# Two layers of a diffusion backbone on one core: adaLN sums on three elementwise engines instead of fp32 strip matmuls

## Chip, cores and metric

The kernel runs on one core of one Trainium2 chip. The metric is the device time of one execution in microseconds; given are the median and the range of three runs. A profile is one execution recorded by the hardware profiler. PE is TensorE (its matmuls) and PEld its weight loads, DVE is VectorE, ACT is ScalarE, POOL is GpSimd, SP is SyncE, which issues most DMAs.

## What is computed

512 latent tokens and 256 context tokens, 1024 wide, go through two layers in fp32. Each layer forms shift, scale and gate from a conditioning vector (adaLN), normalises its input, projects it, mixes tokens by attention, gates with SiLU, projects out and adds the result to the stream.

```python
def adaln(cvec, w, b):
    m = jax.nn.silu(cvec) @ w + b
    return jnp.split(m, 3, axis=-1)

for i in range(DEPTH):                      # DEPTH = 2
    shift, scale, gate = adaln(c, ada_w[i], ada_b[i])
    cshift, cscale, cgate = adaln(c_ctx, ada_w[i], ada_b[i])
    h = rms_norm(x, pre_g[i]) * (1.0 + scale) + shift
    hc = rms_norm(xc, pre_g[i]) * (1.0 + cscale) + cshift
    # i = 0: differential attention, 8 heads; i = 1: grouped-query attention, 8 heads, 2 kv heads
    x = x + gate * rms_norm(y, post_g[i])
    # layer 0 only: xc = xc + cgate * rms_norm(yc, post_g[i])
```

The part that the change touches is the product of the two vectors silu(c) and silu(c_ctx) with `ada_w`: 1024 rows in, 3072 columns out, for each layer. The columns are taken in sections of 512: 0 and 1 are shift, 2 and 3 scale, 4 and 5 gate. The projections and attention products are written as three products of a high and a low part (hi*hi, hi*lo, lo*hi), in a rounded fp32 form that TensorE takes in one pass.

## The kernel before

Layer 0's shift and scale are made first, since the first projections need them; this part stays as it is. While layer 0's heads run, the kernel makes six more sections in the order of the tuple `SECS`: layer 0's gate (0,4) and (0,5), then layer 1's shift and scale (1,0), (1,2), (1,1), (1,3). Layer 1's gate is made later, in layer 1's heads, by running sums on DVE (`gate1_part`, L1598: acc = row tile times a scalar per partition, plus acc) and a column sum on PE (`colsum`, L406 and L407).

Each of the six sections was made in two groups. `grp_load` (L826) fetches four k tiles of 128 x 512, 1 MB in one DMA on SP's queue, into one buffer `araw`. `grp_mm` (L836) multiplies each of the four by a 128 x 32 block `s32`, whose first two columns are the two vectors, so that the four results lie in four strips of 32 partitions of one PSUM bank. These are true fp32 matmuls, two passes each. The first group of a section is copied to `arow` by ACT (L839), the second added by DVE (L842). Then `gate0_finish` (gate) splits the row in a high and a low part (L1128, L1129) and multiplies by a selector `selb` that picks one vector's row out of each strip, adds them and spreads them over all partitions (L1132, L1134); `ada1_finish` (shift, scale) transposes four 128 x 128 blocks on PE (`row_cols`, L532), adds the strips on DVE (L536) and writes `mods`.

The order of the work comes from a planner. `flow` holds streams of steps with due times: scores and softmax (`S_`), transposes of p (`T_`), p times v (`M_`), sub-layer norms (`X_`), and the adaLN steps (`A_`). It runs what is due on a clock of estimated costs, and fills up with pieces of the projections from `fillq`. `ACCN` says how many adaLN steps belong to each head. The constants at the head of the file (lags, priorities, orders of projections, choice of engine) feed it, and a scheduler then places every instruction in its engine's queue, which runs in order.

For one tile of 128 queries in layer 0, per head: PE writes scores to PSUM (L995), DVE takes the maximum (L1000), ACT the exponential p (L1003), DVE the reciprocal of the sum (L1006), GpSimd scales the first map's p (L233), DVE adds the second map's with its factor (L1011), PE transposes p (L1060), ACT and DVE split it into ah and al (L1063, L1064), PE multiplies by v (L167). Weights come through `raw` buffers on SP's queue (L223), are rounded to whi by ACT (L225) and their rests wlo made by DVE (L219).

Of the kernel before, what the change touches and what calls it, by code (L numbers as in the profile page):

```python
# [61 lines left out]
EHL = ('vvvvvvvv', 'pppppppp')
EWL = ('vp', 'vp', 'pp', 'pp')
XF = (0, 0, 0)
FL = (2, 3, 2)
RB = 1
# [21 lines left out]
def tile_backbone(  # L88
# [401 lines left out]
    sel32 = cp.tile([P, 2], F32, name="sel32", bufs=1)  # L490
    nc.vector.tensor_reduce(sel32, ident.rearrange("p (j r) -> p r j", j=4)[:, 0:2, :], AX.X, ALU.add)
    selb = [cp.tile([P, P], F32R, name=f"selb{v}", bufs=1) for v in range(2)]
    for v in range(2):
        nc.vector.tensor_copy(selb[v], sel32[:, v:v + 1].to_broadcast([P, P]))
# [33 lines left out]
    def row_cols(r, n):  # L528
        o = scb[:, 0, :n * P] if seq else trp()[:, :n * P]
        for b in range(n):  # L530
            with after(seq[0] if seq else None):
                i = nc.tensor.transpose(o[:, b * P:(b + 1) * P], r[:, b * P:(b + 1) * P], ident)  # L532
# [3 lines left out]
        nc.vector.tensor_reduce(  # L536
            cols_.rearrange("p (b r) -> p b r", b=n), o.rearrange("p (b j r) -> p b r j", j=4, r=32)[:, :, 0:2, :], AX.X, ALU.add)
        return cols_
# [277 lines left out]

    with tc.tile_pool(name="t0", bufs=1) as t0:
        SECS = ((0, 4), (0, 5), (1, 0), (1, 2), (1, 1), (1, 3))
        groups = [(layer, sec, g) for layer, sec in SECS for g in range(2)]
        loaded, rows = {}, {}  # L820

        def grp_load(i):
            if i < len(groups):
                layer, sec, g = groups[i]
                t = loaded[i] = t0.tile([P, 4, 512], F32, tag="araw", name=nm("araw"), bufs=1)
                nc.sync.dma_start(  # L826
                    t, ada_w[layer, g * 512:(g + 1) * 512, sec * 512:(sec + 1) * 512].rearrange("(k p) n -> p k n", p=P))

        def grp_mm(i):
            layer, sec, g = groups[i]  # L830
            t = loaded.pop(i)
            o = trp()
            prev = None
            for j in range(4):
                with onward(prev):
                    prev = nc.tensor.matmul(o[32 * j:32 * j + 32, :], s32[:, 4 * g + j, :], t[:, j, :], start=True, stop=True)  # L836
            if g == 0:
                r = rows[layer, sec] = t0.tile([P, 512], F32, tag="arow", name=nm("arow"), bufs=1)
                nc.scalar.copy(r, o)  # L839
            else:  # L840
                r = rows[layer, sec]
                nc.vector.tensor_tensor(r, o, r, ALU.add)  # L842
            grp_load(i + 1)

        def ada1_finish(layer, sec):
            r = rows.pop((layer, sec))
            ov_ = row_cols(r, 4).rearrange("p (k v) -> p v k", v=2)
            mod_cols(layer, sec % 2, sec // 2, lambda v: ov_[:, v, :])
# [271 lines left out]
        gate0 = [hp.tile([P, D], F32, name=f"gate0_{v}", bufs=1) for v in range(2)]  # L1120

        def gate0_finish(half):
            r = rows.pop((0, 4 + half))
# [3 lines left out]
            rh, rl = (t0.tile([P, 512], F32R, tag="tmp", name=nm("rg"), bufs=3) for _ in range(2))  # L1127
            nc.scalar.copy(rh, r)  # L1128
            nc.vector.tensor_tensor(rl, r, f32(rh), ALU.subtract)  # L1129
            for v in range(2):  # L1130
                o = trp()
                nc.tensor.matmul(o, selb[v], rh, start=True, stop=False)  # L1132
                with tc.high_priority(offset=3000):
                    nc.tensor.matmul(o, selb[v], rl, start=False, stop=True)  # L1134
# [31 lines left out]
            add({"qk": qk_proj, "v": v_proj, "z": z_proj}[kind](i))  # L1166
        def acc_steps():
            res = []
            grp_load(0)
            for i, (layer, sec, g) in enumerate(groups):  # L1170
                res.append(Step(lambda i=i: grp_mm(i), 1.5, hot=False))
                if g:
                    f = (lambda sec=sec: gate0_finish(sec - 4)) if layer == 0 else (lambda layer=layer, sec=sec: ada1_finish(layer, sec))
                    res.append(Step(f, 2.0 if layer == 0 else 1.0, [(res[-1], ACD)], hot=False))
# [637 lines left out]
```

## Time and profile before

| what | value |
|---|---|
| runs, median (range) | 787.72 us (787.7 to 788.16) |
| profiled execution, first to last instruction | 786.1 us |
| PE busy | 771.3 us |
| PEld busy | 683.3 us |
| DVE busy | 526.6 us |
| ACT busy | 452.0 us |
| POOL busy | 321.8 us |
| granted TensorE clock, mean | 0.998 |

A line of the profile names the source line, the engine, the operation, `out<-in` by the program's names, the shape, and the count; behind the bar stand the busy time in us, the mean of one instruction in ns, and the idle time of the engine just before such instructions with what ended it. In a wait, `A <- B` means that A waited for B, with the total in us, how often, and the longest. In the timeline a line is the start, the duration, and merged instructions of one kind. Layer 0's heads run from about 80 to 455 us, its output projection to about 515, layer 1 from there to the end.

### The profile page before, as it was taken

To read this page: it belongs to the slowest core of one execution; us is meant where nothing else is said; L and a number is where in the kernel's file an instruction comes from. 1 tells how busy PE (TensorE), PEld (TensorE's weight loads), DVE (VectorE), ACT (ScalarE), POOL (GpSimd) and SP (SyncE) were. 2 spreads that over 40 slices of the span, in tenths; PEclk is the share of its full clock that TensorE was granted. 3 is DMA by queue.
4 is the path that set the end of the run, shared out by engine and by line. 5 is a ranking of instruction groups with operands and counts; after the bars stand their busy time and mean duration, and the time that the engine had idled before them with its cause. 6 is when DMAs were issued, how large, how long until landed. Compare 5 with 4: busy or idle time off the path is not lost.

```text
span 786.1 us, 13615 instructions
## 1 busy us (share of the span) xinstructions
PE 771.3 (98%) x5158; PEld 683.3 (87%) x5158; DVE 526.6 (67%) x934; ACT 452.0 (58%) x982; POOL 321.8 (41%) x428
## 2 busy tenths in 40 slices
PE   8999999999999999999999999999999999999996
PEld 6689888989888998988979888887999999989986
DVE  4666676886879747867578735667568987665634
ACT  5546546674576644774468724654466676666632
POOL 1121364663346542453425402574545555234102
PEclk9999999999999999999999999999999999999999
DMA  9925211230142421312520133031423512100102
GB/s 339 387 80 202 74 55 42 68 134 28 48 151 84 148 82 68 90 71 95 173 96 29 53 148 121 1 113 59 157 81 103 157 39 80 51 31 28 54 28 107
DMA packets 34065, 77.72 MB, mean 99 GB/s; under 512 B 3408, under 2 KB 8016, under 8 KB 34000
## 3 DMA queue, kind: packets, MB, share of 16 engines
q1 hardware_dynamic: 30144, 71.05, 26.9%
q10 hardware_dynamic: 3856, 5.81, 2.1%
q8 instruction: 40, 0.66, 0.3%
q14 instruction: 25, 0.20, 0.1%
HBM read 70.56 MB, written 2.10 MB: 92 GB/s over the span
## 4 chain that ended last, share of the span: by engine, by line
PE 93%; DVE 3%; ACT 3%; DMA 1%; issue 1%; POOL 0%; SPq 0%; DVEq 0%; ACTq 0%
PE bk L155 57%; PE sc L155 11%; PE bk L167 9%; PE sc L995 5%; PE bk L1060 3%; PE bk L1552 3%; PE bk L836 1%; PE sc L1024 1%; DMA xnt<-in_xlT 1%; ACT p L1003 1%; PE bk L406 1%; PE sc L1348 1%; PE bk L407 0%; PE bk L1488 0%; DVE wlo L219 0%
## 5 line engine op out<-in xcount | busy, mean ns | idle before, releaser
L155 PE MATMUL bk<-h,whi 128*128 128x512 f32 (+2 forms) x864 | 228.3, 347 | 0.0
L155 PE MATMUL bk<-whi,h 128*128 128x256 f32 (+1 forms) x992 | 226.0, 317 | 1.4 <-DVE kl L1422 1.4
L155 PEld LDWEIGHTS bk<-whi,h 128*128 128x128 f32 x992 | 165.8, 190 | 17.4 <-issue 3.2
L155 PEld LDWEIGHTS bk<-h,whi 128*128 128x128 f32 x864 | 149.9, 189 | 17.1 <-issue 3.3
L155 PE MATMUL bk<-wlo,h 128*128 128x256 f32 (+1 forms) x496 | 155.5, 315 | 0.0
L155 PE MATMUL bk<-h,wlo 128*128 128x512 f32 (+2 forms) x432 | 148.5, 345 | 0.0
L233 POOL TENSOR_SCALAR p<-p,sm 128x768 f32<-128x768 f32 (+1 forms) x80 | 70.5, 884 | 160.1 <-DVE sm L1006 72.9
L219 DVE TENSOR_TENSOR wlo<-raw,whi 128x1024 fp32r<-128x1024 f32 (+1 forms) x66 | 81.9, 1243 | 39.9 <-ACT whi L225 38.1
L155 PEld LDWEIGHTS bk<-wlo,h 128*128 128x128 f32 x496 | 94.0, 190 | 6.1 <-issue 0.7
L225 ACT CAST whi<-raw 128x1024 fp32r<-128x1024 f32 x64 | 67.1, 1049 | 52.0 <-PE bk L155 32.4
L155 PEld LDWEIGHTS bk<-h,wlo 128*128 128x128 f32 x432 | 81.3, 189 | 7.7 <-issue 1.1
L1003 ACT ACTIVATE p<-sc,sm 128x768 f32<-128x768 f32 (+1 forms) x68 | 59.5, 878 | 38.8 <-DVE sm L1000 38.5
L1000 DVE TENSOR_REDUCE sm<-sc 128x1 f32<-128x768 f32 (+1 forms) x68 | 60.3, 917 | 18.5 <-PE sc L995 18.3
L219 POOL TENSOR_TENSOR sz<-sz,za 128x192 f32<-128x192 f32 (+1 forms) x48 | 34.8, 745 | 68.4 <-ACT za L199 68.3
L1064 DVE TENSOR_TENSOR al<-bk,ah 128x512 fp32r<-128x512 f32 x56 | 37.3, 683 | 10.5 <-ACT ah L1063 10.3
L995 PE MATMUL sc<-qk,qk 64*128 64x384 f32 (+1 forms) x396 | 43.6, 350 | 0.7 <-ACT p L1003 0.7
L1011 DVE SCALAR_TENSOR_TENSOR p<-p,sm,p 128x768 f32<-128x768 f32 (+1 forms) x34 | 39.9, 1175 | 4.0 <-POOL p L233 1.6
L1556 DVE TENSOR_TENSOR al<-bk,ah 128x512 fp32r<-128x512 f32 x48 | 32.1, 685 | 15.5 <-ACT ah L1555 15.3
L995 PEld LDWEIGHTS sc<-qk,qk 64*128 64x128 f32 x396 | 32.8, 184 | 7.9 <-issue 3.1
L1537 ACT ACTIVATE p<-sc,sm,qrs 128x768 f32<-128x768 f32 x32 | 31.9, 998 | 11.6 <-PE bk L1552 5.2
L1063 ACT CAST ah<-bk 128x512 fp32r<-128x512 f32 x56 | 31.7, 590 | 11.6 <-PE bk L1060 10.0
L1555 ACT CAST ah<-bk 128x512 fp32r<-128x512 f32 x48 | 27.1, 589 | 18.7 <-PE bk L1552 17.4
(241 smaller groups left out, 1503.5 us busy)
## 6 DMA issues: line engine op xcount, KB each, us to landing
raw<-in_a_w SPq DMA_DIRECT2D x28, 512.0 KB, 3.6
araw<-in_ada_w SPq DMA_DIRECT2D x12, 1024.0 KB, 5.1
raw<-in_b_w SPq DMA_DIRECT2D x20, 512.0 KB, 3.5
ag<-in_ada SPq DMA_DIRECT2D x16, 512.0 KB, 7.8
raw<-in_w_out SPq DMA_DIRECT2D x16, 512.0 KB, 3.5
sw<-qr ACTq DMA_DIRECT2D x32, 128.0 KB, 2.1
gw<-in_ada_w SPq DMA_DIRECT2D x8, 512.0 KB, 3.8
xnt<-in_xlT SPq DMA_DIRECT2D x4, 512.0 KB, 5.7
```

Of the source, the lines that this page charges most:

```text
L155: i = nc.tensor.matmul(o, a, b, start=start, stop=stop)
L167: nc.tensor.matmul(o, v[:, kt + e, c], a[:, e * 256:e * 256 + 256], start=first and i == 0, stop=last and i == 5)
L219: eng.tensor_tensor(dst[:, i:i + n], a[:, i:i + n], b[:, i:i + n], op)
L225: nc.scalar.copy(hi, r)
L233: (nc.vector if eng == "v" else nc.gpsimd).tensor_scalar(dst, src, s_, 1.0, ALU.mult, ALU.mult)
L995: prev = nc.tensor.matmul(sc[m][:, j if nk == T else m, :w], a[r, tok], b[r, c], start=i == 0, stop=i == 2)
L1000: nc.vector.tensor_reduce(mx, scv, AX.XY if nk == T else AX.X, ALU.max, negate=True)
L1003: nc.scalar.activation(pv_, scv, AF.Exp, bias=mx, accum_out=l[:, m:m + 1])
L1011: nc.vector.scalar_tensor_tensor(ps_[0], pt, r, ps_[0], ALU.mult, ALU.add)
L1064: nc.vector.tensor_tensor(al, tr, f32(ah), ALU.subtract)
L1537: nc.scalar.activation(pt.rearrange("p (j n) -> p j n", j=2), scv, AF.Exp, scale=sr, bias=nmx, accum_out=l)
L1556: nc.vector.tensor_tensor(al, tr, f32(ah), ALU.subtract)
```

## The change

The six sections are no longer made by matmuls. Each comes in four parts of two k tiles (512 KB, two buffers, the load two parts ahead). For either vector `v` there is an accumulator of 128 x 512, to which every k tile times its scalar per partition is added. For the first vector all eight tiles go on DVE (one scaling, seven multiply-adds). For the second, the first tile goes on DVE, and each of the other seven is scaled in place by ACT and added by GpSimd. The sum over the 128 partitions is left to the finish. `gate0_finish` does it with `colsum` (all ones instead of the selector); the low part is now made by GpSimd. `sec_finish` transposes 32 x 32 blocks of the accumulator on DVE and reduces them, which leaves 16 numbers per partition in `rall`; when the last section is there, one fp32 matmul with `msel`, a mask and one more reduction give the columns of all four sections, and `mods` is written.

```diff
+EACC = ('dddddddd', 'daaaaaaa')
-                t = loaded[i] = t0.tile([P, 4, 512], F32, tag="araw", name=nm("araw"), bufs=1)
+                t = loaded[i] = t0.tile([P, 2, 512], F32, tag="araw", name=nm("araw"), bufs=2)
...
-            for j in range(4):
-                with onward(prev):
-                    prev = nc.tensor.matmul(o[32 * j:32 * j + 32, :], s32[:, 4 * g + j, :], t[:, j, :], start=True, stop=True)
-            if g == 0:
-                r = rows[layer, sec] = t0.tile([P, 512], F32, tag="arow", name=nm("arow"), bufs=1)
-                nc.scalar.copy(r, o)
-            else:
-                r = rows[layer, sec]
-                nc.vector.tensor_tensor(r, o, r, ALU.add)
+            for k in range(2):
+                k_ = 2 * k2 + k
+                for v in range(2):
+                    acc = sums[layer, sec][v]
+                    s_ = scol[:, v, k_:k_ + 1]
+                    e = EACC[v][k_]
+                    eng = {"d": nc.vector, "p": nc.gpsimd, "a": nc.scalar}[e]
+                    with tc.issue_after(last_of(eng)):
+                        if e == "d" and k_:
+                            eng.scalar_tensor_tensor(acc, t[:, k, :], s_, acc, ALU.mult, ALU.add)
+                            continue
+                        o = t[:, k, :] if k_ else acc
+                        if e == "a":
+                            eng.activation(o, t[:, k, :], AF.Copy, scale=s_)
+                        else:
+                            eng.tensor_scalar(o, t[:, k, :], s_, None, ALU.mult)
+                    if k_:
+                        with tc.issue_after(last_of(nc.gpsimd)):
+                            nc.gpsimd.tensor_tensor(acc, acc, o, ALU.add)
+            part_load(i + 2)
...
+        def sec_finish(layer, sec):
+            idx = 2 * SECS.index((layer, sec)) - 4
+            for v in range(2):
+                tr = t0.tile([P, 512], F32, tag="tmp", name=nm("tr"), bufs=3)
+                with tc.issue_after(last_of(nc.vector)):
+                    nc.vector.transpose(tr, sums[layer, sec][v])
+                    nc.vector.tensor_reduce(rall[:, idx + v, :], tr.rearrange("p (b i) -> p b i", i=32), AX.X, ALU.add)
+            if sec == 3:
+                o = trp()[:, :P]
+                nc.tensor.matmul(o, msel, rall.rearrange("p s b -> p (s b)"), start=True, stop=True)
...
-                nc.tensor.matmul(o, selb[v], rh, start=True, stop=False)
+                colsum(o, sums[0, 4 + half][v], [t0.tile([P, 512], F32R, tag="tmp", name=nm("rg"), bufs=3) for _ in range(2)])
```

The constants are fitted anew, some thirty-five of them. Those that move work between engines: `EG0` (gT scaled by subg, 24 instructions) from DVE to ACT, `EG1` (layer 1's copy of g, 16) from ACT to DVE, `HFD` (one more of four hf tiles on DVE), `KVE` and `EWL` (some wlo). `HF0` puts z projection 6 into the last head, `KV` reorders layer 1's k, v and transposes, `ACCN` is (1, 4, 2, 4, 6, 5, 5, 3) for 30 steps where it was (0, 0, 3, 2, 4, 1, 4, 4) for 18, `NWARM` is 11 and not 12.

PE's queue before, in head 3, around its norm's column sum (sqs); bk are PSUM banks, whi and wlo weights, h the normalised input:

```order
L155 MATMUL bk_68<-wlo_2623,h_279 128x256
L406 MATMUL bk_69<-sqs_2986,ones_r 128x384
L155 MATMUL bk_68<-whi_2622,h_280 128x256
L155 MATMUL bk_68<-whi_2622,h_327 128x256
L155 MATMUL bk_68<-wlo_2623,h_327 128x256
L836 MATMUL bk_70<-araw_2749,s_129 32x512 x4
L407 MATMUL bk_69<-sqs_2987,ones_r 128x384
```

The same column sum of head 3 on PE in the changed kernel:

```order
L156 MATMUL bk_68<-wlo_2671,h_581 128x256
L156 MATMUL bk_68<-whi_2670,h_582 128x256
L407 MATMUL bk_70<-sqs_3109,ones_r 128x384
L156 MATMUL bk_68<-whi_2670,h_591 128x256
L156 MATMUL bk_68<-wlo_2671,h_591 128x256
L156 MATMUL bk_68<-whi_2670,h_592 128x256
L156 MATMUL bk_69<-whi_2537,h_231 128x256
```

The strip group (L836) is gone; projections stand around the column sum as before, others of the same kind.

GpSimd's queue before, in head 3: p is the softmax scaling, qr the rotation of the next head's q and k, sqs the norm's low part:

```order
L233 TENSOR_SCALAR p_2832<-p_2832,sm_2817 128x768
L219 TENSOR_TENSOR qr_2629<-qr_2629,rope 128x256 x2
L219 TENSOR_TENSOR qr_2629<-qr_2629,sw_2776 128x256 x2
L233 TENSOR_SCALAR p_2941<-p_2941,sm_2926 128x768
L405 TENSOR_TENSOR sqs_2980<-sq_2772,sqs_2979 128x384
L233 TENSOR_SCALAR p_3044<-p_3044,sm_3029 128x768
L405 TENSOR_TENSOR sqs_2987<-sq_2772,sqs_2986 128x384
```

GpSimd's queue in head 3 of the changed kernel (L855 is the addition to the second vector's accumulator):

```order
L234 TENSOR_SCALAR p_2933<-p_2933,sm_2918 128x768
L406 TENSOR_TENSOR sqs_3103<-sq_2889,sqs_3102 128x384
L855 TENSOR_TENSOR acc_2829<-acc_2829,araw_2619 128x512 x2
L234 TENSOR_SCALAR p_3017<-p_3017,sm_3002 128x768
L220 TENSOR_TENSOR qr_2871<-qr_2871,rope 128x256 x2
L406 TENSOR_TENSOR sqs_3110<-sq_2889,sqs_3109 128x384
L220 TENSOR_TENSOR qr_2871<-qr_2871,sw_2984 128x256 x2
L855 TENSOR_TENSOR acc_2829<-acc_2829,araw_2835 128x512 x2
L234 TENSOR_SCALAR p_3133<-p_3133,sm_3118 128x768
L855 TENSOR_TENSOR acc_2829<-acc_2829,araw_2950 128x512 x2
L234 TENSOR_SCALAR p_3248<-p_3248,sm_3233 128x768
```

Between two scalings of p there now stands a pair of 512-wide additions, directly ahead of the next scaling.

DVE's queue in the changed kernel, head 3 (L1025 maximum, L1031 reciprocal, L1036 combination of the two maps, L220 rest of a weight tile, L846 the multiply-add to the first vector's accumulator):

```order
L1036 SCALAR_TENSOR_TENSOR p_2933<-p_2939,sm_2918,p_2933 128x768
L846 SCALAR_TENSOR_TENSOR acc_2828<-araw_2619,scol,acc_2828 128x512 x2
L1025 TENSOR_REDUCE sm_3015<-sc_72 128x1
L1025 TENSOR_REDUCE sm_3021<-sc_73 128x1
L1031 RECIPROCAL sm_3002<-sm_3002 128x1
L220 TENSOR_TENSOR wlo_3068<-raw_3065,whi_3067 128x1024
L846 SCALAR_TENSOR_TENSOR acc_2828<-araw_2835,scol,acc_2828 128x512
L1031 RECIPROCAL sm_3002<-sm_3002 128x1
L846 SCALAR_TENSOR_TENSOR acc_2828<-araw_2835,scol,acc_2828 128x512
```

The multiply-adds stand between the steps of the softmax, where before there were none of them.

More of the change, by code (lines that the diff above doesn't have):

```diff
@@ L62 @@
 EHL = ('vvvvvvvv', 'pppppppp')
[L63 to L66, printed above, removed]
+EWL = ('pv', 'vp', 'pp', 'pv')
+XF = (0, 4, 1)
+FL = (0, 1, 3)
+RB = 2
 HFB = 3
-PRI = (1359, 218, 582, 400)
+PRI = (1359, 0, 523, 648)
 GFIN = (10, 13)
-QLAG = 2.87
-QTR = 7.76
-EG0 = 'v'
+QLAG = 2.99
+QTR = 9.24
+EG0 = 'a'
 EP0 = 'p'
@@ L489, in tile_backbone @@
     nc.vector.tensor_copy(s32[:, :, 0:2], scv)
[L490 to L494, printed above, removed]
+    msel = cp.tile([P, 4, 32], F32, name="msel", bufs=1)
+    mask = cp.tile([P, 4], F32, name="mask", bufs=1)
+    nc.vector.tensor_reduce(msel[:, 0, :], ident.rearrange("p (g j) -> p j g", j=32), AX.X, ALU.add)
+    nc.vector.tensor_copy(msel[:, 1:, :], msel[:, 0:1, :].to_broadcast([P, 3, 32]))
+    nc.vector.tensor_reduce(mask, ident.rearrange("p (a r) -> p a r", r=32), AX.X, ALU.add)
+    msel = msel.rearrange("p g j -> p (g j)")
     def quad(cs, o, g):
@@ L818, in tile_backbone @@
         SECS = ((0, 4), (0, 5), (1, 0), (1, 2), (1, 1), (1, 3))
[L819 to L824, printed above, removed]
-                t = loaded[i] = t0.tile([P, 4, 512], F32, tag="araw", name=nm("araw"), bufs=1)
+        parts = [(layer, sec, k2) for layer, sec in SECS for k2 in range(4)]
+        loaded, sums = {}, {}
+        rall = con.tile([P, 8, 16], F32, name="rall")
@@ L826, in grp_load, with part_load @@
+        def part_load(i):
+            if i < len(parts):
+                layer, sec, k2 = parts[i]
+                t = loaded[i] = t0.tile([P, 2, 512], F32, tag="araw", name=nm("araw"), bufs=2)
                 nc.sync.dma_start(
-                    t, ada_w[layer, g * 512:(g + 1) * 512, sec * 512:(sec + 1) * 512].rearrange("(k p) n -> p k n", p=P))
-        def grp_mm(i):
-            layer, sec, g = groups[i]
+                    t, ada_w[layer, k2 * 256:(k2 + 1) * 256, sec * 512:(sec + 1) * 512].rearrange("(k p) n -> p k n", p=P))
@@ L843, in grp_mm @@
[L843 to L848, printed above, removed]
+            if k2 == 0:
+                sums[layer, sec] = [t0.tile([P, 512], F32, tag=f"acc{v}", name=nm("acc"), bufs=1) for v in range(2)]
+            for k in range(2):
[17 more added lines that the diff above has]
+                            nc.gpsimd.tensor_tensor(acc, acc, o, ALU.add)
@@ new lines, in part_sum_ @@
+            part_load(i + 2)
[9 more added lines that the diff above has]
+                nc.tensor.matmul(o, msel, rall.rearrange("p s b -> p (s b)"), start=True, stop=True)
+                om = con.tile([P, 32, 4], F32, name="om")
+                nc.vector.tensor_tensor(om, o.rearrange("p (s a) -> p s a", a=4), mask.unsqueeze(1).to_broadcast([P, 32, 4]), ALU.mult)
+                oc_ = con.tile([P, 4, 2, 4], F32, name="oc")
+                nc.vector.tensor_reduce(oc_.rearrange("p s v k -> p (s v k)"), om, AX.X, ALU.add)
+                for i, (l_, sc_) in enumerate(SECS[2:]):
+                    mod_cols(1, sc_ % 2, sc_ // 2, lambda v: oc_[:, i, v, :])
@@ L1168, in acc_steps @@
             res = []
[L1169 to L1174, printed above, removed]
+            part_load(0)
+            part_load(1)
+            for i, (layer, sec, k2) in enumerate(parts):
+                res.append(Step(lambda i=i: part_sum_(i), 0.0, hot=False))
+                if k2 == 3:
+                    f = (lambda sec=sec: gate0_finish(sec - 4)) if layer == 0 else (lambda layer=layer, sec=sec: sec_finish(layer, sec))
+                    res.append(Step(f, 2.0 if layer == 0 else 0.0, [(res[-1], ACD)], hot=False))
             return res
```

63 lines of the change are left out of this document (29 added, 34 removed).

## The prediction

> **What bounds the kernel now.** I read the page's head first, then the chain, then what TensorE waited for, then the stretches of the span.
>
> ```profile
> span 786.1 us, 13615 instructions
> PE 771.3 (98%) x5158; PEld 683.3 (87%) x5158; DVE 526.6 (67%) x934; ACT 452.0 (58%) x982; POOL 321.8 (41%) x428
> PE 93%; DVE 3%; ACT 3%; DMA 1%; issue 1%; POOL 0%; SPq 0%; DVEq 0%; ACTq 0%
> ```
>
> The reader is to see three things: matmuls cover 98% of the span, the chain that ended last lies on PE for 93% of it, and PE's idle time is 786.1 - 771.3 = 14.8 us in all. All eleven waits of PE for another engine stand in one answer; here are its longest, at the start of the program, and the two that lie in layer 0's heads, where the change is (us in total, times, longest):
>
> ```profile
> PE bk L155 <- DVE sqx L618: 1.8, 3, 1.2
> ...
> PE bk L167 <- DVE al L1064: 1.2, 1, 1.2
> ...
> PE bk L836 <- DVE al L1064: 0.6, 1, 0.6
> ```
>
> The stretches show where the idle time lies (columns: busy time of PE, weight loads, DVE, ACT, POOL):
>
> ```profile
> 0.00:40.00 40.00, 35.56 (x251) 26.12 (x252) 22.53 (x63) 20.83 (x42) 6.26 (x13) 1.00 0.97 358
> 120.00:440.00 320.00, 318.72 (x2296) 281.70 (x2295) 232.02 (x392) 195.71 (x417) 151.81 (x181) 1.00 0.27 88
> 400.00:440.00 40.00, 38.87 (x272) 34.69 (x273) 32.87 (x63) 29.84 (x66) 19.09 (x22) 1.00 0.16 53
> 590.00:636.00 46.00, 46.00 (x339) 44.55 (x338) 41.05 (x78) 30.55 (x67) 21.93 (x27) 1.00 0.43 125
> 760.00:786.00 26.00, 20.06 (x134) 18.41 (x132) 12.43 (x19) 7.26 (x20) 4.76 (x14) 0.94 0.26 94
> ```
>
> The first 40 us (4.4 idle) and the last 26 (5.9) hold most of it. Layer 0's heads, 120 to 440, where all strip matmuls lie, lose 1.3 us in 320. There a microsecond of PE work removed is a microsecond gained, as long as the other engines still keep up. Matmul ends are modelled, so I check with starts:
>
> ```profile
> 184.42 0.40 PE L155 MATMUL bk<-whi,h 128*128 128x256 f32 x2
> 184.66 0.28 PE L155 MATMUL bk<-wlo,h 128*128 128x256 f32 x1
> 184.78 0.28 PE L155 MATMUL bk<-whi,h 128*128 128x256 f32 x1
> ```
>
> Four 256-column matmuls start within 0.36 us, one per 0.12, with no gap: PE is really streaming. [...] The even starts speak for the full amount, which I take.
>
> **What goes from PE.** One strip group and its neighbours, and one finish of a section:
>
> ```profile
> L836 PE MATMUL bk<-araw,s 128*32 128x512 f32 x96 | 12.8, 605 | 0.6 <-DVE al L1064 0.6
> 160.12 0.40 PE L167 MATMUL bk<-al,vhi 128*128 128x256 f32 x2
> 160.45 1.07 PE L836 MATMUL bk<-araw,s 128*32 128x512 f32 x8
> 161.45 0.38 PE L155 MATMUL bk<-whi,h 128*128 128x256 f32 x1
> 161.67 0.28 PE L155 MATMUL bk<-wlo,h 128*128 128x256 f32 x1
> ...
> 302.73 0.40 PE L167 MATMUL bk<-al,vhi 128*128 128x256 f32 x2
> 302.97 0.60 PE L532 MATMUL bk<-ident,arow 128*128 128x128 f32 x4
> 303.50 1.33 PE L995 MATMUL sc<-qk,qk 64*128 64x384 f32 x12
> ```
>
> The two L167 from 160.12 would have been followed at 160.36; L155 starts at 161.45, 1.09 us later, and its successor 0.22 us after it and not 0.12. One group thus holds PE 1.19 us, and the 12 groups 14.3 us (a little over the 12.8 busy). The four transposes of a section's finish hold it from 302.97 to 303.50: 0.53, four finishes 2.1 us. What comes in is one fp32 matmul of 128 columns (two passes), for all four sections together. The nearest row is the warm-up matmul of that shape, and the two rows behind it are gate0's:
>
> ```profile
> L155 PE MATMUL sc<-ones 128*128 128x128 f32 x14 | 2.4, 297 | 0.3 <-DVE sm L536 0.3
> L1132 PE MATMUL bk<-rg,selb 128*128 128x512 f32 x4 | 1.8, 446 | 0.0
> ```
>
> 7 of them in 2.4 us are 0.34 each; I take 0.4. gate0 keeps eight matmuls of the same shape (ones for a selector), so 0. One warm-up matmul less and two fills more lie in the first 40 us, in idle time: 0, and without that cover 0.34 each. Net on PE: 14.3 + 2.1 - 0.4 = 16.0 us.
>
> **What comes to the others.** Layer 1's gate is already made by such sums on DVE; its rows and the nearest others:
>
> ```profile
> L1598 DVE SCALAR_TENSOR_TENSOR gate<-gw,scol,gate 128x512 f32<-128x512 f32 x14 | 12.3, 877 | 0.1
> L1596 DVE TENSOR_SCALAR gate<-gw,scol 128x512 f32<-128x512 f32 x2 | 1.4, 718 | 0.0
> L1030 DVE TENSOR_REDUCE sm<-sc 128x2 f32<-128x512 f32 x14 | 9.4, 683 | 2.1 <-PE sc L1024 2.1
> L233 DVE TENSOR_SCALAR gT<-bk,subg 128x256 f32<-128x256 f32 x24 | 11.5, 477 | 6.3 <-ACT sq L1081 6.3
> L842 DVE TENSOR_TENSOR arow<-bk,arow 128x512 f32<-128x512 f32 x6 | 4.1, 685 | 1.1 <-PE bk L836 0.9
> L1129 DVE TENSOR_TENSOR rg<-arow,rg 128x512 fp32r<-128x512 f32 x2 | 1.7, 840 | 0.0
> L1128 ACT CAST rg<-arow 128x512 fp32r<-128x512 f32 x2 | 1.2, 620 | 2.0 <-DVE arow L842 1.5 <-issue 0.5
> L1081 ACT ACTIVATE sq<-bk 128x256 f32<-128x256 f32 x24 | 9.3, 386 | 4.0 <-PE bk L167 3.9
> L839 ACT COPY arow<-bk 128x512 f32<-128x512 f32 x6 | 3.5, 585 | 2.2 <-PE bk L836 2.2
> L405 POOL TENSOR_TENSOR ac<-gate,ac 128x512 fp32r<-128x512 f32 x2 | 2.6, 1300 | 0.3 <-ACT ac L404 0.2
> L405 POOL TENSOR_TENSOR sqs<-sq,sqs 128x512 fp32r<-128x512 f32 x1 | 1.9, 1885 | 0.1
> ```
>
> DVE: 42 multiply-adds x 0.877 = 36.8; 12 scalings x 0.718 = 8.6; 8 block transposes, which the trace does not show, between 0.68 and 0.88 by the one-input and two-input rows of 128x512, taken at 0.72 = 5.8; 8 reductions x 0.683 = 5.5. Off it go the 24 scalings of gT that move to ACT (11.5), the L842 additions (4.1) and L1129 (1.7). Sum +39.4. ACT: 42 scalings x 0.62 = 26.0, 24 of gT x 0.386 = 9.3, two more casts 1.2, less 3.5: +33.0. GpSimd: 42 adds, between 1.3 and 1.885, taken at 1.5 = 63, and gate0's four low parts x 1.3 = 5.2: +68.
>
> Layer 0's heads then take 320 - 16 = 304 us of PE, beside DVE 232 + 39 = 271 (89%), ACT 196 + 33 = 229 (75%), GpSimd 152 + 68 = 220 (72%). The same load stands in the trace: 590 to 636, with layer 1's running sums, has DVE at 41.05 of 46 (89%) and PE without any idle time. But ACT (66%) and GpSimd (48%) were freer there. In 400 to 440, with DVE at 82% and ACT at 75%, PE lost 1.13 us of 40. So the heads' 304 us lose between 0 and 1.13 x 304/40 = 8.6 us more. I take 2.5, nearer to the first row, because the instruction is the same; this is a choice.
>
> **Waits, and what stands behind them.** On GpSimd an addition to acc now waits for ACT's scaling and for the DMA, and in the new order the softmax scaling of the next query tile stands right behind pairs of them. Who waits for that is the m=1 combination on DVE, then the transposes on PE. On SP a part's load waits until DVE and GpSimd have left its buffer, with the weight loads behind it; before, L826 waited for PE in the same way:
>
> ```profile
> SPq L826 <- PE bk L836: 59.3, 9, 11.8
> ```
>
> Yet none of PE's eleven waits is for a DMA. I cost this at 0 to 2, taken at 0. PSUM: twelve uses of a bank go, worth nothing where PE did not wait.
>
> **The rest of the refit** moves layer 1's copies of g and one more hf tile in four from ACT to DVE, reorders the k and v work, and puts one z projection a head later. From 440 on PE idles 7.8 us, of which 5.9 are the end that no order shortens much. I take 0, bounds -2 to +2.
>
> **Sum.** 786.1 - 16.0 + 2.5 = 772.6 for the span. The median of the runs, 787.72, lies 1.6 above this execution's span; so 774.2, and I forecast **774**. With the bounds: 787.72 - 16.0 - 2 = 769.7 to 787.72 - 16.0 + 8.6 + 1 = 781.3.
>
> **Rivals.**
> First, GpSimd's pairs come late for PE (chance 0.10).
>
> ```profile
> POOL p L233 <- DVE sm L1006: 72.9, 24, 8.6
> ...
> 182.78 1.01 DVE L1011 SCALAR_TENSOR_TENSOR p<-p,sm,p 128x768 f32<-128x768 f32 x1
> 185.89 0.65 PE L1060 MATMUL bk<-ident,p 128*128 128x128 f32 x4
> ```
>
> Here p was ready at 183.79 and read at 185.89: 2.1 us of cover. A pair of adds takes 2.6 at least. If each of the 24 parts reaches PE with the 0.5 left over, 12 us come back: 787.72 - 16 + 12 = 783.7. Against it: GpSimd waited 72.9 us for DVE in front of that scaling, so it has gaps to put pairs in.
>
> Second, on the other side: DVE and GpSimd hold each other up and DVE becomes the bound (0.08). Layer 1's sums show it:
>
> ```profile
> L1598 DVE SCALAR_TENSOR_TENSOR gate<-gw,scol,gate x14: 726/749/1477, 591.9 to 633.5; 128x512 f32<-128x512 f32 x14
> ```
>
> Median 0.749, longest 1.477. At 1.477 for all 42, DVE has 271 + 25 = 296 us; 89% is the highest DVE share at which the trace shows a PE without waits, and 296/0.89 = 333 us of heads instead of 320 make 787.7 + 13 = 801. It decides from 0.89 x 321.6 = 286 us of DVE work on, that is from a mean of 1.24 us. For it: GpSimd has 45% more work to collide with. Against it: 0.877 is a mean that already holds collisions. [...]
>
> Third, the freed PE time is no gain because PE's order, not its work, sets the pace (0.02): 787. The even starts speak against it. Fourth, the refit removes waits as well, below 769.5 (0.04).
>
> **How the numbers follow.** My own case has 0.76, with 769.7 to 781.3. The range, 769.5 to 783, adds about half of the first rival. Faster by over 0.2% (below 786.1; about what a measurement can tell here) gets the own case, the first and the fourth rival, less a little for a first rival that grows: 0.88. Within 0.2%: 0.04, the third rival and that remainder. Slower: 0.08.
>
> **What would show it.** In the changed profile: PE's busy time near 771.3 - 15 = 756, no strip group; the multiply-add row of acc near 0.88 us (over 1.24 the second rival); GpSimd's adds 1.3 to 1.9 us; DVE near 89% from 120 to 424 with PE's idle time there below 10 us. I am wrong if PE's waits for al, p or acc in layer 0's heads sum to over 8 us, or if layer 1 moves by more than 2.

## The result and the profile after

The changed kernel takes 806.38 us (median of four runs, 804.15 to 807.43) where the kernel before takes 787.82: a ratio of 1.0231, interval 1.0216 to 1.0247, 18.6 us slower. The forecast was 774, the far end of its range 783. One execution of one kernel below, the one with the gate's low part on DVE, took 2657 us; its median is that of the other three.

The head of its page and the chain:

```profile
span 803.7 us, 13614 instructions
PE 770.5 (96%) x5050; PEld 685.1 (85%) x5050; DVE 583.9 (73%) x991; ACT 475.6 (59%) x1022; POOL 395.6 (49%) x476
PE 26%; DVE 3%; POOL 1%; ACT 1%; DMA 1%; issue 0%; DVEq 0%; ACTq 0%; POOLq 0%
```

PE's idle time is 803.7 - 770.5 = 33.2 us where it was 14.8, and its busy time has not fallen although it holds 108 matmuls fewer (5050 for 5158). The chain's shares add up to a third of the span only, so it says little here. The stretch of layer 0's heads that the prediction argued from (columns as there; then granted clock, DMA share, GB/s):

```profile
120.00:440.00 320.00, 302.55 (x2092) 270.67 (x2089) 264.60 (x388) 212.38 (x448) 214.66 (x217) 0.98 0.27 85
```

PE lost 1.3 us there before and loses 17.4 now, at a mean clock of 0.98 instead of 1.00. DVE is at 264.60 of 320, 83%: not full. The starts of the context scores of heads 0 to 6 show how the loss gathers:

| us | 0 | 1 | 2 | 3 | 4 | 5 | 6 | last transposes of p | last matmul |
|---|---|---|---|---|---|---|---|---|---|
| before | 107 | 148 | 185 | 231 | 277 | 336 | 379 | 446 | 780 |
| after | 107 | 159 | 199 | 245 | 299 | 347 | 396 | 471 | 797 |

The distance is 0, 11, 14, 14, 22, 11 and 17 us at the heads, 25 at the last transposes of layer 0 and 17 at the end. It does not grow evenly, since projections stand between the heads in another order (a z projection is now in the last one). The 8 us that come back are not layer 1's: from the first transposes of its p to the last matmul it takes 192.9 us before and 193.8 after. They lie between the two attentions, 140.9 us before and 132.8 after. One planner constant moved by 0.1 in the kernel before (ATT, below) makes this stretch 149.1 us with the total only 1.5 us longer, so these marks do not tell how much work is done by then. What PE waited for, longest first, with one line further down:

```profile
PE sc L1020 <- ACT p L1028: 3.5, 3, 2.1
PE bk L156 <- DVE al L1089: 3.4, 3, 1.7
PE bk L408 <- POOL rg L406: 3.3, 2, 2.7
...
PE bk L1085 <- DVE al L1089: 1.2, 2, 1.0
...
PE bk L168 <- DVE al L1089: 1.0, 3, 0.6
```

No wait is large; they are many and short. The waits for al and p in the heads come to 3.5 + 3.4 + 1.2 + 1.0 = 9.1 us, over the 8 at which I said I would be wrong. The longest single one, of 2.7 us, shows how a short wait becomes a long loss. The timeline there (PE, DVE and POOL):

```profile
143.71 4.79 POOL L855 TENSOR_TENSOR acc<-acc,araw 128x512 f32<-128x512 f32 x3
145.92 1.25 DVE L1035 TENSOR_TENSOR sm<-sm,nlam 128x1 f32<-128x1 f32 x1
147.27 2.04 DVE L1036 SCALAR_TENSOR_TENSOR p<-p,sm,p 128x768 f32<-128x768 f32 x1
147.32 0.49 PE L407 MATMUL bk<-rg,ones_r 128*128 128x512 f32 x1
148.46 1.98 POOL L406 TENSOR_TENSOR rg<-acc,rg 128x512 fp32r<-128x512 f32 x1
150.49 0.50 PE L408 MATMUL bk<-rg,ones_r 128*128 128x512 f32 x1 [2.68 <-POOL rg L406]
151.75 1.01 PE L156 MATMUL bk<-h,whi 128*128 128x384 f32 x2 [0.55 <-ACT qr L892]
152.56 0.52 PE L156 MATMUL bk<-h,wlo 128*128 128x384 f32 x1
152.88 0.84 PE L156 MATMUL bk<-h,whi 128*128 128x384 f32 x2
```

Two stretches of 4 us of the same place:

```profile
148.00:152.00 4.00, 0.95 (x3) 0.52 (x4) 3.81 (x5) 1.78 (x4) 4.00 (x4) 0.86 0.41 131
152.00:156.00 4.00, 4.00 (x13) 4.00 (x14) 3.42 (x5) 1.09 (x3) 1.83 (x2) 0.50 0.40 131
```

Three additions hold GpSimd for 4.79 us. Behind them stands the low part of the gate's row (rg), 1.98 us long; PE's second column sum (L408) needs it and stands at the head of PE's queue, so nothing on PE starts for 2.68 us. Meanwhile a multiplication of 128 numbers takes DVE 1.25 us (mean before: 0.253) and the combination of p 2.04. Then the granted clock falls to 0.50: the 384-column matmuls start 0.32 us apart (152.56 to 152.88), where the commonest distance of such matmuls in this trace is 0.175. Three slices of 40 us hold such falls, where before all slices from 120 to 440 had 1.00:

```profile
120.00:160.00 40.00, 35.64 (x217) 30.54 (x215) 31.23 (x41) 22.68 (x46) 25.56 (x21) 0.91 0.19 60
...
240.00:280.00 40.00, 36.79 (x245) 31.88 (x244) 31.96 (x47) 26.31 (x58) 29.57 (x30) 0.96 0.32 103
...
360.00:400.00 40.00, 35.66 (x258) 31.67 (x258) 34.28 (x51) 25.17 (x50) 29.22 (x28) 0.96 0.38 119
```

They lose up to (0.09 + 0.04 + 0.04) x 40 = 6.8 us of full-speed time by the clock alone (up to, because PE stood idle in a little of it).

### The profile page after: what moved, and what is told of

It reads as the page before. It is cut to its first block, busy times and chain, and to the rows that moved or that the text cites. A ratio compares the mean times of both kernels' runs of the same rounds, so it can differ in the third digit from the quotient of the medians.

```text
span 803.7 us, 13614 instructions
## 1 busy us (share of the span) xinstructions
PE 770.5 (96%) x5050; PEld 685.1 (85%) x5050; DVE 583.9 (73%) x991; ACT 475.6 (59%) x1022; POOL 395.6 (49%) x476
## 5 line engine op out<-in xcount | busy, mean ns | idle before, releaser
L156 PEld LDWEIGHTS bk<-h,whi 128*128 128x128 f32 x864 | 153.8, 192 | 20.4 <-DVE al L1089 4.1
L156 PE MATMUL bk<-h,wlo 128*128 128x512 f32 (+2 forms) x432 | 151.7, 351 | 0.0
L220 DVE TENSOR_TENSOR wlo<-raw,whi 128x1024 fp32r<-128x1024 f32 (+2 forms) x65 | 85.3, 1314 | 35.3 <-ACT whi L226 34.5
L855 POOL TENSOR_TENSOR acc<-acc,araw 128x512 f32<-128x512 f32 x42 | 61.9, 1474 | 27.1 <-ACT araw L850 16.2
L220 POOL TENSOR_TENSOR sz<-sz,za 128x192 f32<-128x192 f32 (+1 forms) x48 | 33.3, 714 | 73.4 <-ACT za L200 73.4
L1025 DVE TENSOR_REDUCE sm<-sc 128x1 f32<-128x768 f32 (+1 forms) x68 | 60.4, 915 | 8.3 <-PE sc L1020 8.3
L850 ACT ACTIVATE araw<-araw,scol 128x512 f32<-128x512 f32 x42 | 30.2, 727 | 38.5 <-DVE acc L846 30.8
L1036 DVE SCALAR_TENSOR_TENSOR p<-p,sm,p 128x768 f32<-128x768 f32 (+1 forms) x34 | 44.4, 1305 | 7.2 <-POOL p L234 4.9
L1089 DVE TENSOR_TENSOR al<-bk,ah 128x512 fp32r<-128x512 f32 x56 | 37.5, 682 | 9.7 <-ACT ah L1088 9.5
L846 DVE SCALAR_TENSOR_TENSOR acc<-araw,scol,acc 128x512 f32<-128x512 f32 x42 | 42.4, 1009 | 2.7 <-DMA araw<-in_ada_w 2.4
L220 POOL TENSOR_TENSOR qk<-qr,qk 128x256 fp32r<-128x256 f32 x42 | 35.8, 884 | 13.6 <-ACT qk L915 7.7
```

Of the source, the lines that this page charges most:

```text
L156: i = nc.tensor.matmul(o, a, b, start=start, stop=stop)
L220: eng.tensor_tensor(dst[:, i:i + n], a[:, i:i + n], b[:, i:i + n], op)
L846: eng.scalar_tensor_tensor(acc, t[:, k, :], s_, acc, ALU.mult, ALU.add)
L855: nc.gpsimd.tensor_tensor(acc, acc, o, ALU.add)
L1025: nc.vector.tensor_reduce(mx, scv, AX.XY if nk == T else AX.X, ALU.max, negate=True)
L1036: nc.vector.scalar_tensor_tensor(ps_[0], pt, r, ps_[0], ALU.mult, ALU.add)
```

## The experiments

Kernels are timed against the kernel before, run beside them (medians 787.65 to 787.81 us). The theories at the start: the loss lies in the work of the sums (DVE's load, GpSimd's additions with what stands behind and beside them, or the queue in which ACT's scaling in place waits for DVE and GpSimd for ACT), or in the refitted constants, or PE's pace is set by something else than its work, so that freed PE time is worth nothing. Later runs set two more against each other: that the freed time is there but only for an order of work that fits (order theory), and that something holds the kernel in any order (floor theory).

**Constants or sums?** First, the sums with the constants of before, but for the number of adaLN steps for each head:

```diff
-ACCN = (0, 0, 3, 2, 4, 1, 4, 4)
+EACC = ('dddddddd', 'daaaaaaa')
+ACCN = (0, 0, 5, 4, 6, 2, 7, 6)
```

> The changed kernel's sums with the constants of before (steps per head scaled from 18 to 30). Load theory (the sums' own work on DVE, ACT and GpSimd delays what PE waits for, whatever the constants): 798 to 812 us, with waits of PE for al, p or rg in layer 0's heads and stretches of half clock. Refit theory (the new constants space the work too tightly; the sums hide behind looser ones): 772 to 780 us.

Then the strips with the new constants:

```diff
-ACCN = (1, 4, 2, 4, 6, 5, 5, 3)
+ACCN = (1, 2, 1, 3, 3, 3, 3, 2)
```

> The strip matmuls of before with the new constants (steps per head scaled from 30 to 18). Load theory: 785 to 793 us, close to the kernel before. Refit theory: the loss of 33 us stays and the strip matmuls come on top, 812 to 822 us.

Measured: 823.03 us (1.0443, 1.0427 to 1.0458) and 796.18 (1.0108, 1.0091 to 1.0125). The new constants help the sums by 16.6 us and hurt the strips by 8.4. With the constants held, the sums in place of the strips cost 823.0 - 787.8 = 35.3 us with the old set and 806.4 - 796.2 = 10.2 with the new one. The constants are not the cause, and they are worth far more than the 0 I gave them: each set is fitted to its own work.

**Which of the sums?** Steps after the first k tile are left out, for both vectors, the second, or the first; each kernel has one of the three marked lines:

```diff
                 for v in range(2):
+                    if k_:                 # no sums
+                    if v == 1 and k_:      # no second vector (ACT, GpSimd)
+                    if v == 0 and k_:      # no first vector (DVE)
+                        continue
```

> The changed kernel with only the first k tile of each section scaled; the other seven tiles of both vectors are loaded but not added (left out of the computation), so 42 multiply-adds on DVE, 42 scalings on ACT and 42 additions on GpSimd are gone while PE's work and the constants stay. Load theory: 787.8 - 16 = 772, 769 to 777. Refit theory: still over 795.

> The changed kernel without the second vector's sums beyond the first k tile (left out of the computation): 42 scalings on ACT and 42 additions on GpSimd are gone, the first vector's 42 multiply-adds on DVE stay. [...] Refit theory: over 795.

> The changed kernel without the first vector's 42 multiply-adds on DVE (left out of the computation); the second vector's 42 scalings on ACT and 42 additions on GpSimd stay. Queue theory (ACT scales a tile in place and so waits until DVE has read it, 30.8 us in the changed kernel, with the softmax behind it; without DVE's reading this wait goes): 788 to 794, as without any sums. [...]

Measured: 790.89 us (1.0038, 1.0023 to 1.0053), 789.82 (1.0029, 1.0017 to 1.0041) and 800.39 (1.0162, 1.0145 to 1.0179). DVE's 42 multiply-adds alone cost nothing (beside the second vector's part they cost 806.4 - 800.4 = 6.0); the second vector's part costs 806.4 - 789.8 = 16.6. But even without any sum the kernel stays above the 787.8 of before, 17 us over the forecast: two losses, not one.

Next, ACT's scalings stay and only GpSimd's 42 additions go:

```diff
-                    if k_:
-                        with tc.issue_after(last_of(nc.gpsimd)):
-                            nc.gpsimd.tensor_tensor(acc, acc, o, ALU.add)
```

> The changed kernel without GpSimd's 42 additions for the second vector (left out of the computation); ACT's 42 scalings and DVE's 42 multiply-adds stay. Queue theory (ACT stands behind DVE's reading, 30.8 us): still 800 or more. [...]

Measured: 788.69 us (1.0012, 1.0003 to 1.0022). In this order the additions cost 17.7 us, and ACT's scalings nothing. Of the runs that leave sums out this one is nearest to the changed kernel: counted in the traces, 207 of PE's 5050 matmuls lie outside the longest sequence that both share, where without any sums it is 575. With another order of both (ATT at 13.62, below) the additions cost 811.8 - 800.4 = 11.4. The groups of DVE in the changed kernel:

```profile
L220 DVE TENSOR_TENSOR wlo<-raw,whi 128x1024 fp32r<-128x1024 f32 x61 | 82.6, 1355 | 34.7 <-ACT whi L226 34.5
L1036 DVE SCALAR_TENSOR_TENSOR p<-p,sm,p 128x768 f32<-128x768 f32 x32 | 43.2, 1349 | 7.1 <-POOL p L234 4.9
L846 DVE SCALAR_TENSOR_TENSOR acc<-araw,scol,acc 128x512 f32<-128x512 f32 x42 | 42.4, 1009 | 2.7 <-DMA araw<-in_ada_w 2.4
L1035 DVE TENSOR_TENSOR sm<-sm,nlam 128x1 f32<-128x1 f32 x34 | 14.7, 431 | 0.8
```

The same groups without the additions:

```profile
L220 DVE TENSOR_TENSOR wlo<-raw,whi 128x1024 fp32r<-128x1024 f32 x61 | 81.0, 1329 | 34.1 <-ACT whi L226 33.9
L846 DVE SCALAR_TENSOR_TENSOR acc<-araw,scol,acc 128x512 f32<-128x512 f32 x42 | 37.7, 898 | 3.9 <-DMA araw<-in_ada_w 3.7
L1033 DVE SCALAR_TENSOR_TENSOR p<-p,sm,p 128x768 f32<-128x768 f32 x32 | 36.6, 1144 | 7.7 <-POOL p L234 5.4
L1032 DVE TENSOR_TENSOR sm<-sm,nlam 128x1 f32<-128x1 f32 x34 | 9.8, 289 | 0.9
```

All four groups are longer beside the additions: 1.6 + 6.6 + 4.7 + 4.9 = 17.8 us of DVE time in these four groups. That it comes out like the loss shows nothing by itself, since not all of it need be on the path.

Is it this lengthening, or the additions' place in GpSimd's queue? Two memsets instead of each addition occupy GpSimd and read nothing:

```diff
-                            nc.gpsimd.tensor_tensor(acc, acc, o, ALU.add)
+                            for _ in range(2):
+                                nc.gpsimd.memset(o, 0.0)
```

> The changed kernel with two GpSimd memsets of the scaled 128x512 tile in place of each of the 42 additions (the second vector's sums are left out of the computation). They stand in the same queue and wait for ACT in the same way, but read nothing. [...]

The additions of the changed kernel:

```profile
L855 POOL TENSOR_TENSOR acc<-acc,araw 128x512 f32<-128x512 f32 x42 | 61.9, 1474 | 27.1 <-ACT araw L850 16.2 <-issue 9.4 <-PE bk L408 0.5
```

The memsets in their place:

```profile
L856 POOL MEMSET araw<- 128x512 f32 x84 | 43.0, 525 | 29.4 <-ACT araw L850 27.6
```

DVE's rows beside the memsets:

```profile
L846 DVE SCALAR_TENSOR_TENSOR acc<-araw,scol,acc 128x512 f32<-128x512 f32 x42 | 37.2, 885 | 4.1 <-DMA araw<-in_ada_w 3.9
L1037 DVE SCALAR_TENSOR_TENSOR p<-p,sm,p 128x768 f32<-128x768 f32 x32 | 35.3, 1104 | 5.5 <-POOL p L234 3.1
```

Measured: 796.46 us (1.0111, 1.0095 to 1.0128). DVE's durations are back (885 and 1104 ns; the 128x1 multiplication 306), yet 7.8 of the 17.7 us stay; GpSimd's queue is the likely reason. The other 9.9 went with the additions, by the end of DVE's lengthening and by 61.9 - 43.0 = 18.9 us less on GpSimd; this run does not part these two. PE's order moved as well: 398 matmuls lie outside the sequence shared with the changed kernel, where ATT alone moves 293 and 5.4 us. So 7.8 and 9.9 are readings in one order, not prices.

**Other places for the sums.** All on DVE; ACT's scalings into a tile of their own, so that they no longer wait for DVE to leave the buffer; and the gate's low part from GpSimd to DVE:

```diff
-EACC = ('dddddddd', 'daaaaaaa')
+EACC = ('dddddddd', 'dddddddd')
```

> The changed kernel with the second vector's sums on DVE too: 84 multiply-adds there, none of the 42 scalings on ACT and 42 additions on GpSimd. DVE gets 42 x 0.75 to 1.0 = 32 to 42 us more, 87 to 93% of layer 0's heads. Queue theory (the hand-over from DVE to ACT to GpSimd is the cost, DVE's own adds are nearly free as without the second vector): 788 to 798. Load theory for DVE (89% is the limit): over 806.

```diff
-                        o = t[:, k, :] if k_ else acc
+                        o = t0.tile([P, 512], F32, tag="asc", name=nm("asc"), bufs=1) if k_ else acc
```

> The changed kernel with ACT scaling into a tile of its own (one buffer) and not in place, so that ACT waits for GpSimd's last addition but no longer for DVE. Everything is still computed. Queue theory: the 30.8 us that ACT stood behind DVE's multiply-adds go, 790 to 799. Load theory for GpSimd: 803 to 809; the single buffer can hold ACT behind GpSimd, which would also keep it there.

```diff
-        nc.gpsimd.tensor_tensor(lo, src, f32(hi), ALU.subtract)
+        (eng or nc.gpsimd).tensor_tensor(lo, src, f32(hi), ALU.subtract)   # eng: nc.vector for gate0
```

> The changed kernel with the four low parts of layer 0's gate made by DVE and not by GpSimd. In the changed profile PE waits 3.3 us for them and the clock falls to half for 6.8 us behind the first. If that is a loss of its own: 806.4 - 3.3 - 3.4 = 800, 797 to 802. If another wait takes its place: 804 to 808.

Measured: 807.94 us (1.0263, 1.0225 to 1.0302), 812.48 (1.0314, 1.0298 to 1.0329) and 808.17 (1.0263, 1.0246 to 1.028). None helps. On DVE the second vector's sums cost 807.9 - 789.8 = 18.1 us, about as much as the 16.6 on ACT and GpSimd: the loss does not belong to GpSimd alone. With the gate's low part on DVE, PE's stop for it did not go:

```profile
PE bk L408 <- DVE rg L406: 3.6, 2, 3.2
```

The low part now stands behind DVE's multiplication of 128 numbers and combination of p, which took 1.25 and 2.04 us in the changed kernel's timeline above, beside the same additions. With a tile of its own ACT's wait moves from DVE's multiply-add to GpSimd's addition. The changed kernel's wait (us, times, longest):

```profile
ACT araw L850 <- DVE acc L846: 30.8, 21, 4.1
```

The wait with a tile of its own:

```profile
ACT asc L850 <- POOL acc L855: 37.2, 14, 8.9
```

That scaling in place is the cause falls with this, and with the 788.69 above, where it stays and costs nothing.

**Is freed PE time worth anything?** In the kernel before, each strip group becomes one matmul of 128 columns, some 9.5 us of PE work less, with every transfer and finish kept:

```diff
-            for j in range(4):
-                with onward(prev):
-                    prev = nc.tensor.matmul(o[32 * j:32 * j + 32, :], s32[:, 4 * g + j, :], t[:, j, :], start=True, stop=True)
+            prev = nc.tensor.matmul(o[:, :128], s32[:, 0:4, :].rearrange("p a b -> p (a b)"), t[:, 0, :128], start=True, stop=True)
```

> The kernel before with its own constants and planner costs, where each strip group of four matmuls of 512 columns is one matmul of 128 columns (the sums are left out of the computation). PE holds 12 x (1.19 - 0.4) = 9.5 us less. Work theory (in layer 0's heads PE's work sets the pace): 787.8 - 9.5 = 778, 776 to 781. Pace theory (the heads are paced by the chain of softmax, transposes and splits, and the strip matmuls filled time that PE had to wait anyway): 784 to 788.

Measured: 787.46 us (0.9998, 0.9988 to 1.0007), no gain at all. It was 7 us ahead at head 6 (372 and not 379) and lost that in the last head. The same kernel with another order, by a lag of the planner's (`ATT` 15.15 to 15.25) or the group's cost in it:

```diff
-ATT = 15.15
+ATT = 15.25
```

> The kernel before with small matmuls in place of the strips (sums left out) and ATT 15.25 for 15.15, another order of the same work. Pace theory: 785 to 792 again. Order theory: a scatter of several us, between 777 and 797.

```diff
-                res.append(Step(lambda i=i: grp_mm(i), 1.5, hot=False))
+                res.append(Step(lambda i=i: grp_mm(i), 0.5, hot=False))
```

> The kernel before with small matmuls in place of the strips (sums left out), the planner told that a group costs 0.5 and not 1.5, so that its clock runs 12 us shorter; 2316 of PE's rows stand elsewhere. Pace theory: 785 to 792. Order theory: anything between 777 and 800; below 783 would show that the freed time can be had.

Measured: 780.81 us (0.9917, 0.9903 to 0.9932) and 781.14 (0.992). 7.0 and 6.7 of the 9.5 are there for the taking once the order fits (PE's busy time fell by 7.6 and 9.4 us, and by 6.2 in the run without gain); that PE's freed time can't be had falls. What does an order alone do? The kernel before with `ATT` 15.25 and with another lag changed:

```diff
-ATT = 15.15
+ATT = 15.25
```

> The kernel before with one planner constant moved by 0.1 (ATT 15.15 to 15.25, the planned length of a head). No instruction is added or removed; 626 of PE's 4559 rows stand elsewhere. Order theory (the order of before is a narrow optimum; nearly any other order makes PE wait, and that, not the sums alone, costs what the freed PE time should have given): 790 to 800 us. Work theory: within 1 us of 787.8.

```diff
-SLAG = (4.74, 1.08)
+SLAG = (4.84, 1.08)
```

> The kernel before with another planner constant moved by 0.1 (SLAG 4.74 to 4.84, the distance between two softmax steps); 1889 of PE's rows stand elsewhere, the work is the same. Order theory: 790 to 800 us. Work theory: within 1 us of 787.8.

Measured: 789.23 us (1.0019, 1.001 to 1.0029) and 799.58 (1.0145, 1.0128 to 1.0162). A tenth in one planner constant, with no work added, costs 11.8 us. The longest wait of PE in that kernel:

```profile
PE bk L155 <- ACT qr L867: 2.2, 1, 2.2
```

The stretch in which that wait ends (at 140.92), and two more behind it:

```profile
140.00:144.00 4.00, 3.08 (x15) 3.08 (x16) 3.41 (x7) 2.70 (x6) 4.00 (x5) 0.64 0.00 2
...
152.00:156.00 4.00, 2.71 (x21) 2.35 (x22) 3.47 (x6) 2.91 (x7) 3.36 (x5) 0.84 0.68 253
156.00:160.00 4.00, 3.10 (x11) 2.70 (x10) 3.23 (x8) 2.99 (x10) 4.00 (x7) 0.50 0.00 0
```

It is the picture of the changed kernel again: a wait of some 2 us, then matmuls at half the clock. The changed kernel in another order, and the same shift without GpSimd's additions and without any sums:

```diff
-ATT = 13.52
+ATT = 13.62
```

> The changed kernel, nothing left out, with ATT 13.62 for 13.52: 892 of PE's rows stand elsewhere. If the constants of the changed kernel are a narrow optimum too: 808 to 820. If the sums alone set its time: 804 to 808.

> As the run without GpSimd's 42 additions (788.7 us), with the planner's constant ATT at 13.62, which puts many PE rows into another order and changes no work. Order theory (the freed PE time is lost to an order that does not fit, so another order gives another time): anywhere between 776 and 798, and more than 3 us away from 788.7. Floor theory (something that no order removes holds the kernel at about 789 once the strips are out): 787 to 791.

> As the run with the sums left out but for the first k tile (790.9 us), with the planner's constant ATT at 13.62. Order theory: between 772 and 798, and more than 3 us away from 790.9. Floor theory: 789 to 793. Neither theory lets it be below 771, which is the time before less the PE work removed.

Measured: 811.78 us (1.0313, 1.0295 to 1.033), 800.37 (1.0164, 1.0147 to 1.0181) and 790.59 (1.0043, 1.003 to 1.0056). Without the additions the order alone costs 11.7 us again; without sums it moved 247 of PE's 5050 matmuls and no time, where the order theory had promised over 3 us. So an order can lose 12 us in this form too, but none that was tried gains: that the missing time is there for the taking in the changed form is shown for the strips only. It stays open.

## Why the prediction was wrong

**"There a microsecond of PE work removed is a microsecond gained"** failed, and this is the first half of the loss: without any sums 790.9 and not 772 to 774. Two kernels with about the same PE busy time tell it. The page of the one without sums begins:

```profile
span 789.3 us, 13424 instructions
PE 764.2 (97%) x5050; PEld 682.0 (86%) x5050; DVE 531.0 (67%) x949; ACT 451.0 (57%) x980; POOL 330.2 (42%) x434
```

The page of the kernel before with small matmuls, in the order that fits:

```profile
span 779.0 us, 13474 instructions
PE 763.7 (98%) x5086; PEld 685.1 (88%) x5086; DVE 528.6 (68%) x934; ACT 450.9 (58%) x982; POOL 321.7 (41%) x428
```

The second keeps PE's idle time at 15.3 us, the first has 25.1. In the first, PE is busy for 7.1 us less than in the kernel before, about half of what was taken out. With the new constants held, strips out and no sums in give 796.2 - 790.9 = 5.3 us. Even starts of matmuls prove that PE streams at that place in that order. They do not prove that the next matmul is ready a microsecond earlier when something in front of it goes. The likely reason is that p, al and qr come from chains on DVE, ACT and GpSimd that do not get shorter; the runs show that the order decides how much is gained (0.3, 7.0 or 6.7 us for the same edit), not which chain holds PE. The third rival said that the order sets the pace, 787 us, and I gave it 0.02 on the strength of those starts.

The size was nearly right. From the first strip matmul to the next other one, every one of the 12 groups took 1.0 us; with the wider gaps ahead of it and behind (0.21 and 0.22 us at 160 us, where 0.12 is usual) 1.19, as predicted. The four transposes took 0.53, 0.35, 0.36 and 0.36, where I had multiplied the longest by four: 14.3 + 1.6 - 0.4 = 15.5, not 16.0.

**"So the heads' 304 us lose between 0 and 1.13 x 304/40 = 8.6 us more. I take 2.5"** was the largest mis-sized term. PE's listed idle time grew by 18.4 us, and 6.8 went at half the clock, which no term held. The row it leaned on, 590 to 636, had DVE at 89% but GpSimd at 48%, and PE waited for nothing there; in the heads GpSimd is now at 214.66 of 320, 67%, and in the stretch shown above without a pause. GpSimd's share is not the whole of it. With all sums on DVE the heads are close to that row on both counts, DVE at 87% and GpSimd at 52%, and PE loses 17.1 us all the same:

```profile
120.00:440.00 320.00, 302.86 (x2101) 272.87 (x2100) 278.25 (x425) 187.03 (x405) 167.12 (x176) 0.98 0.28 85
```

A row of layer 1 does not carry over to layer 0's heads by its shares, whatever engine they are of. The upper bound was also added up too low: 781.3 holds 1 us for the refit and the waits on SP, for which I had bounds of 2 each, so 784.3. The result lies beyond either.

**The costs of the instructions** were mostly right. An addition took 1.474 us (1.5 taken), a block transpose 0.698 (0.72), a multiply-add 1.009 (0.877), a scaling on ACT 0.727 (0.62). DVE's load grew by 57.3 us and not 39.4, GpSimd's by 73.8 (68), ACT's by 23.6 (33). Of DVE's miss of 17.9 us, 5.5 are the multiply-adds and 6.1 the 34 small multiplications of p's factor (431 ns against 253): I asked what the new instructions cost, not what they do to their neighbours.

**"I take 0, bounds -2 to +2"** for the refit failed both ways: -16.6 with the sums, +8.4 with the strips (for the whole refit, layer 0's constants with it). Layer 1 itself moved by under 2 us, as forecast (192.9 and 193.8 us, above).

**The rivals.** The first had the right engine and nearly the right price (12 us; the additions cost 17.7), but added it to a gain that was not there, and looked for it at p alone; the longest stop is the gate's low part, queued behind three additions, and taking that off GpSimd gains nothing. The second gave the nearest time, 801, for a reason that did not decide: the multiply-add stayed under its 1.24 us and DVE was 83% busy. The longer DVE instructions that it rests on are there (1349 ns for the combination of p, 1144 without the additions) as a part of the 9.9 us.

In sum, from the span before: 786.1 - 15.5 + 18.4 (idle) + 6.8 (clock) + 3.1 (the wider spacing below) = 798.9 of 803.7; 4.8 us I could not place. They are not the additions': the run without these has a mean clock of 1.00 from 120 to 440 us, 771.3 - 15.5 + 3.1 = 758.9 us of PE work by the same sum, and 763.7 measured, 4.8 more again.

## What to carry to other kernels

Where a profile shows PE at 98%, removed PE work is a gain only if what PE does next is ready sooner (of 9.5 us removed here, one order gained 0.3 and another 7.0): follow the chain that feeds it through the other engines, and cost what goes into their queues ahead of it. An order fitted to one set of work is part of the kernel's speed: before a change is judged, move the order by a hair, and if that alone moves the time by over 1%, as here, no single time of an edit tells what the edit costs. Long GpSimd instructions can be paid twice: here PE waited 2.68 us for what was queued behind three of them, and four groups of DVE instructions took 17.8 us longer with the 42 additions than without. And look at the clock behind a wait of PE: behind that of 2.68 us it was 0.50 for 6.83 us.

## What the hardware showed

**The clock.** The three falls to 0.50 in the heads of the changed kernel, each with the 3.41 us ahead of it (columns as above):

```profile
147.46:150.87 3.41, 0.73 (x3) 0.31 (x3) 3.41 (x3) 1.10 (x3) 3.41 (x3) 1.00 0.48 154
150.87:157.70 6.83, 6.28 (x21) 5.95 (x20) 4.35 (x7) 2.22 (x6) 2.96 (x3) 0.50 0.23 77
246.45:249.86 3.41, 2.02 (x14) 1.42 (x13) 3.41 (x5) 2.10 (x5) 2.68 (x3) 1.00 0.30 114
249.86:253.27 3.41, 3.41 (x18) 3.31 (x17) 1.27 (x2) 0.52 (x1) 3.41 (x6) 0.50 0.02 5
376.15:379.56 3.41, 1.31 (x12) 0.89 (x12) 2.39 (x6) 3.22 (x7) 3.41 (x4) 1.00 0.00 0
379.56:382.98 3.42, 3.42 (x19) 2.98 (x16) 3.32 (x5) 1.79 (x5) 0.83 (x1) 0.50 0.41 95
```

They last 3.41 or 6.83 us, and their beginnings lie 98.99 and 228.69 us apart, 29 and 67 times 3.413. In the 3.41 us ahead of a fall PE was busy for 0.73, 2.02 and 1.31 us, so it was not idle throughout. At 0.50 each 3.41 us lose up to half, 1.7 us of full-speed time (my estimate). What sets off a fall was not shown.

**DVE beside GpSimd.** DVE's combination of p (128x768) took 1349 ns on average in the kernel with the additions, 1104 with the memsets, 1144 with neither. In proportion the 128x1 multiplication grew the most of the four groups above, 431 ns against 289. The timeline of the changed kernel shows one:

```profile
153.17 1.28 POOL L406 TENSOR_TENSOR rg<-acc,rg 128x512 fp32r<-128x512 f32 x1 [0.62 <-ACT rg L405]
153.20 1.27 DVE L1035 TENSOR_TENSOR sm<-sm,nlam 128x1 f32<-128x1 f32 x1
```

The multiplication begins 0.03 us behind GpSimd's instruction and ends 0.02 us behind its end. The one at 145.92 us in the timeline further up ends 0.02 us behind the end of the addition beside it. Of the 21 multiplications by nlam in that trace that began with more than 0.2 us of a GpSimd instruction left, 20 ended within 0.03 us behind its end; the 13 that began beside none took 0.15 us on average. Why the ends fall together was not shown.

**The spacing of wide matmuls.** Two rows of the timeline of the kernel before, 21 matmuls of 512 columns apart:

```profile
108.91 0.39 PE L155 MATMUL bk<-h,wlo 128*128 128x512 f32 x1
...
113.68 0.39 PE L155 MATMUL bk<-h,wlo 128*128 128x512 f32 x1
```

Two rows of the changed kernel's, 21 apart too:

```profile
109.39 0.40 PE L156 MATMUL bk<-h,wlo 128*128 128x512 f32 x1
...
114.27 0.39 PE L156 MATMUL bk<-h,wlo 128*128 128x512 f32 x1
```

4.77/21 = 0.227 us and 4.88/21 = 0.232. In layer 1 (from 500 us on) the commonest distance is 0.227 in both. The group `sc<-whi,h`, half of it such matmuls, has a mean of 341 ns in the changed kernel, without the additions and with all sums left out, and 337 in the kernel before and in that with small matmuls. Over the 586 such matmuls of the changed kernel's first 500 us the wider spacing costs some 3.1 us. So it is not the load of the sums; where the tiles lie in SBUF was not tried, and the cause stays open.
